# Contrast adjustment on one core: 6 MB tiles of 48 KB rows in place of 4 MB tiles of 32 KB rows, with the clip moved to VectorE

## The chip, the cores and the metric

The kernel runs on one core of a Trainium2 chip. A core has TensorE (matrix products), VectorE, ScalarE and GpSimd (elementwise work and reductions), SyncE (here only an issuer of transfers), and 16 DMA engines that move data between HBM, the chip's memory, and SBUF, the core's own memory of 128 partitions. The metric is the device time of one execution in microseconds, as a median over runs. Lower is better.

## The reference

The input is 48 images (16 batches of 3 channels) of 512 x 512 float32 values. Each image is stretched around its own mean and clipped:

```python
def reference(x, factor):                       # factor = 1.5
    mean = np.mean(x, axis=(2, 3), keepdims=True)
    return np.clip(mean + factor * (x - mean), 0, 1).astype(np.float32)
```

So each output value is clip(factor * x + bias, 0, 1) with bias = (1 - factor) * mean, one bias per image. An image's bias needs the whole image first. Input and output are 50.33 MB each.

## The kernel before

The input is taken as one long row of numbers and cut into 12 tiles of 4 MB. A tile has 128 partitions with 8192 contiguous values each (ROW, 32 KB), so one image covers 32 partitions and a tile holds four whole images. A ring of six such tiles (BUFS) lies in SBUF; tile t lives in buffer t % 6, is changed in place, and is stored from there.

For each tile, `compute(t)` does the following. VectorE sums the first 4352 columns of every partition (L78), while ScalarE sums the other 3840 with an activation that has an accumulator and writes its copy to a scratch tile, junk (L82). TensorE multiplies both sums with a block matrix, blockw, that adds up the 32 partitions of each image and scales by (1 - factor) / pixels (L86, L87); every partition of an image gets its image's bias in PSUM. VectorE copies it to SBUF (L89). Then, in two chunks of 5120 and 3072 columns, ScalarE does relu(factor * x + bias), and VectorE takes the minimum with 1 (L93, L94). Tile 0 has three chunks, and its first 2048 columns are stored on their own.

Loads are issued by SyncE's queue (SP), stores by ScalarE's queue, in the order of the program. SP first issues the loads of the first six tiles: tile 0 in two pieces (1 MB and 3 MB), tile 1, then tiles 2 and 3 together, and 4 and 5 together. From then on it issues load t + 6 behind `compute(t)`; that load waits until store t, which empties its buffer, is complete. ScalarE's store waits for VectorE's last minimum of the tile, and behind it in ScalarE's order are the sums of the next tile. Nothing is ordered by a scheduler: the schedule is manual.

Of the kernel before, what the change touches and what calls it, by code (L numbers as in the profile page):

```python
# [1 line left out]

# [4 lines left out]


P = 128  # L10
ROW = 8192
BUFS = 6
CHUNKS = (5120, 3072)
SHORT = 2048
FIRST = (SHORT, 3072, 3072)
SUM = 4352


@with_exitstack
def kernel(  # L20
    ctx: ExitStack,
    tc: tile.TileContext,
    x: bass.AP,
    factor: float,
    out: bass.AP,
):


    nc = tc.nc
    f32 = mybir.dt.float32  # L30
    Alu = mybir.AluOpType
    Act = mybir.ActivationFunctionType

    B, C, H, W = x.shape
    n_img, n_pix = B * C, H * W
    ppi = n_pix // ROW
    per_tile = P // ppi
    n_tiles = n_img // per_tile
    assert ppi * ROW == n_pix and per_tile * n_tiles == n_img

    factor = float(factor)
    wconst = (1.0 - factor) / float(n_pix)

    x_f = x.rearrange("b c h w -> (b c h w)")
    out_f = out.rearrange("b c h w -> (b c h w)")

    def dram(ap, t, c0=0, c1=ROW):
        return bass.AP(tensor=ap.tensor, offset=t * P * ROW + c0, ap=[[ROW, P], [1, c1 - c0]])

    consts = ctx.enter_context(tc.tile_pool(name="consts", bufs=1))  # L50
    xpool = ctx.enter_context(tc.tile_pool(name="xpool", bufs=1))
    jpool = ctx.enter_context(tc.tile_pool(name="jpool", bufs=1))
    rpool = ctx.enter_context(tc.tile_pool(name="rpool", bufs=2))
    bpool = ctx.enter_context(tc.tile_pool(name="bpool", bufs=2))
    psum = ctx.enter_context(tc.tile_pool(name="psum", bufs=2, space=bass.MemoryType.PSUM))

    blockw = consts.tile([P, P], f32, name="blockw")
    nc.gpsimd.memset(blockw, 0.0)  # L58
    for a in range(0, P, ppi):
        nc.gpsimd.memset(blockw[a : a + ppi, a : a + ppi], wconst)  # L60


    ring = xpool.tile([P, BUFS, ROW], f32, name="ring")

    def load(t, c0=0, c1=ROW, n=1):

        b = t % BUFS
        src = bass.AP(
            tensor=x_f.tensor,
            offset=t * P * ROW + c0,  # L70
            ap=[[ROW, P], [P * ROW, n], [1, c1 - c0]],
        )
        nc.sync.dma_start(out=ring[:, b : b + n, c0:c1], in_=src)  # L73

    def compute(t):
        xt = ring[:, t % BUFS, :]
        sums = rpool.tile([P, 2], f32, name="sums")
        nc.vector.tensor_reduce(  # L78
            out=sums[:, 0:1], in_=xt[:, 0:SUM], axis=mybir.AxisListType.X, op=Alu.add
        )  # L80
        junk = jpool.tile([P, ROW - SUM], f32, name="junk")
        nc.scalar.activation(  # L82
            out=junk, in_=xt[:, SUM:ROW], func=Act.Copy, accum_out=sums[:, 1:2]
        )
        pbias = psum.tile([P, 1], f32, name="pbias")
        nc.tensor.matmul(pbias, blockw, sums[:, 1:2], start=True, stop=False)  # L86
        nc.tensor.matmul(pbias, blockw, sums[:, 0:1], start=False, stop=True)  # L87
        bias = bpool.tile([P, 1], f32, name="bias")
        nc.vector.tensor_copy(out=bias, in_=pbias)  # L89
        c = 0  # L90
        for n in FIRST if t == 0 else CHUNKS:
            part = xt[:, c : c + n]
            nc.scalar.activation(out=part, in_=part, func=Act.Relu, bias=bias, scale=factor)  # L93
            nc.vector.tensor_scalar(out=part, in0=part, scalar1=1.0, scalar2=None, op0=Alu.min)  # L94
            if t == 0 and c == FIRST[0]:
                store(t, 0, c)
            c += n
        store(t, FIRST[0] if t == 0 else 0, ROW)

    def store(t, c0, c1):  # L100
        nc.scalar.dma_start(out=dram(out_f, t, c0, c1), in_=ring[:, t % BUFS, c0:c1])

    with tc.manual_schedule():
        load(0, c1=SHORT)
        load(0, c0=SHORT)
        load(1)
        load(2, n=2)
        load(4, n=2)
        for t in range(n_tiles):
            compute(t)  # L110
            if t + BUFS < n_tiles:
                load(t + BUFS)


# [1 line left out]
_INS = ['x', 'factor']  # L116
_OUTS = [((16, 3, 512, 512), 'float32')]

_NUMBERS = {'factor': 1.5}


# [26 lines left out]
```

## Time and profile before

| what | value |
|---|---|
| median of 7 runs | 239.43 us (239.22 to 239.69) |
| profiled execution, its own time | 239.6 us |
| span in the profile | 237.7 us |
| busy in the span: ScalarE / VectorE / TensorE / GpSimd | 131.1 / 111.9 / 14.0 / 0.9 us |
| moved by DMA | 50.33 MB read, 50.33 MB written, 423 GB/s over the span |
| load queue (q1) / store queue (q10), share of the 16 DMA engines | 49.6% / 49.1% |
| first compute / last store issued | 12.86 us / 217.66 us |

The span is the part of the execution that the profile covers; the rest of the time lies around it. A row of the profile's groups reads: line, engine, operation, output <- input with shapes, count, then the busy time in us and the mean of one in ns, then the idle time of that engine just before, with what ended it. The slices cut the span in 40 equal parts, about 5.9 us each, and a digit is the busy share in tenths. A landing is the time from the issue of a transfer to its completion.

### The profile page before, as it was taken

The page shows a single profiled execution, that of the slowest core. Times are in us where ns is not written, and L with a number is a line of the kernel's source. Part 1 is how long each engine was busy: PE and PEld are TensorE (multiplying, and loading weights), DVE is VectorE, ACT ScalarE, POOL GpSimd, SP SyncE. Part 2 cuts the span into 40 slices and gives each one's busy share as a digit, 9 for nine tenths or more (in the row PEclk, how much of TensorE's full clock was granted, in tenths as well). Part 3 has the DMA queues.
Part 4 walks back from the last instruction along what each step waited for, and adds up shares of the span by engine and source line. Part 5 has one row for each costly group of instructions (what it writes and reads, how often), then busy time and mean ns, then how long its engine had stood idle before and what let it go on. Part 6 is the DMA issues. An engine that isn't in the chain of part 4 may idle for free.

```text
span 237.7 us, 307 instructions
## 1 busy us (share of the span) xinstructions
PE 14.0 (6%) x48; PEld 12.0 (5%) x48; DVE 111.9 (47%) x49; ACT 131.1 (55%) x50; POOL 0.9 (0%) x9
## 2 busy tenths in 40 slices
PE   0010010001010001010010100100100100100000
PEld 0010010001010001010010100100100100100000
DVE  0073846162864343782928739273462643716000
ACT  2058678056679046769676796753671690593000
POOL 1000000000000000000000000000000000000000
DMA  7999999999999999999999999999999999999996
GB/s 288 418 441 441 418 441 354 459 433 442 436 441 436 425 408 425 436 441 441 441 436 441 436 436 430 408 420 441 436 436 441 441 436 436 441 425 413 419 441 265
DMA packets 3713, 100.67 MB, mean 423 GB/s; under 512 B 384, under 2 KB 384, under 8 KB 384
## 3 DMA queue, kind: packets, MB, share of 16 engines
q1 hardware_dynamic: 1840, 50.33, 49.6%
q10 hardware_dynamic: 1872, 50.33, 49.1%
q14 instruction: 1, 0.01, 0.0%
HBM read 50.33 MB, written 50.33 MB: 423 GB/s over the span
## 4 chain that ended last, share of the span: by engine, by line
DMA 57%; DVE 19%; ACT 10%; another core or an unknown queue 3%; issue 1%; PE 1%; SPq 1%; ACTq 0%
DMA ring<-in_x_dram 40%; DMA out_dram<-ring 17%; ACT ring L93 10%; DVE ring L94 9%; DVE sums L78 9%; PE pbias L87 1%; SPq L73 1%; DVE bias L89 0%; ACTq L93 0%
## 5 line engine op out<-in xcount | busy, mean ns | idle before, releaser
L93 ACT ACTIVATE ring<-ring,bias 128x3072 f32<-128x3072 f32 (+2 forms) x25 | 87.9, 3564 | 22.1 <-DVE bias L89 13.2
L94 DVE TENSOR_SCALAR ring<-ring 128x3072 f32<-128x3072 f32 (+2 forms) x25 | 54.3, 2209 | 56.1 <-ACT ring L93 56.1
L78 DVE TENSOR_REDUCE sums<-ring 128x1 f32<-128x4352 f32 x12 | 56.2, 4683 | 41.5 <-DMA ring<-in_x_dram 41.5
L82 ACT ACTIVATE junk<-ring 128x3840 f32<-128x3840 f32 x12 | 40.8, 3402 | 61.9 <-DMA ring<-in_x_dram 48.6
L86 PE MATMUL pbias<-sums,blockw 128*128 128x1 f32 x24 | 7.0, 361 | 190.3 <-ACT junk L82 190.3
L86 PEld LDWEIGHTS pbias<-sums,blockw 128*128 128x128 f32 x24 | 6.0, 311 | 191.2 <-ACT junk L82 174.7
L87 PE MATMUL pbias<-sums,blockw 128*128 128x1 f32 x24 | 7.0, 362 | 3.9 <-DVE sums L78 3.4
L87 PEld LDWEIGHTS pbias<-sums,blockw 128*128 128x128 f32 x24 | 6.0, 310 | 5.0 <-DVE sums L78 5.0
L89 DVE COPY bias<-pbias 128x1 f32<-128x1 f32 x12 | 1.9, 158 | 8.1 <-PE pbias L87 8.1
L82 ACT ACTIVATION_READ_ACCUMULATOR junk<-ring 128x1 f32 x12 | 2.2, 186 | 0.0
L82 ACT ACT_TABLE_LOAD x1 | 1.3, 1283 | 0.7 <-PEq L129 0.7
L60 POOL MEMSET blockw<- 32x32 f32 x4 | 0.5, 117 | 0.2
L58 POOL MEMSET blockw<- 128x128 f32 x1 | 0.2, 204 | 0.3 <-POOLq L129 0.3
L129 POOL MEMSET const-bfloat16-1.0<- 128x1 bf16 x1 | 0.1, 111 | 0.0
L129 POOL MEMSET const-uint8-127<- 128x1 uint8 x1 | 0.1, 111 | 0.0
L129 POOL MEMSET const-float32-1.0<- 128x1 f32 x1 | 0.1, 108 | 0.0
L129 POOL MEMSET const-float32-0.0<- 128x1 f32 x1 | 0.1, 103 | 0.2 <-issue 0.2
## 6 DMA issues: line engine op xcount, KB each, us to landing
out_dram<-ring ACTq DMA_DIRECT2D x11, 4096.0 KB, 37.9
ring<-in_x_dram SPq DMA_DIRECT2D x7, 4096.0 KB, 46.9
ring<-in_x_dram SPq DMA_DIRECT2D x2, 8192.0 KB, 65.7
ring<-in_x_dram SPq DMA_DIRECT2D x1, 3072.0 KB, 11.7
out_dram<-ring ACTq DMA_DIRECT2D x1, 3072.0 KB, 29.8
ring<-in_x_dram SPq DMA_DIRECT2D x1, 1024.0 KB, 4.8
out_dram<-ring ACTq DMA_DIRECT2D x1, 1024.0 KB, 18.8
```

The lines of the kernel that those rows point to most:

```text
L58: nc.gpsimd.memset(blockw, 0.0)
L60: nc.gpsimd.memset(blockw[a : a + ppi, a : a + ppi], wconst)
L73: nc.sync.dma_start(out=ring[:, b : b + n, c0:c1], in_=src)
L78: nc.vector.tensor_reduce(out=sums[:, 0:1], in_=xt[:, 0:SUM], axis=mybir.AxisListType.X, op=Alu.add)
L82: nc.scalar.activation(out=junk, in_=xt[:, SUM:ROW], func=Act.Copy, accum_out=sums[:, 1:2])
L86: nc.tensor.matmul(pbias, blockw, sums[:, 1:2], start=True, stop=False)
L87: nc.tensor.matmul(pbias, blockw, sums[:, 0:1], start=False, stop=True)
L89: nc.vector.tensor_copy(out=bias, in_=pbias)
L93: nc.scalar.activation(out=part, in_=part, func=Act.Relu, bias=bias, scale=factor)
L94: nc.vector.tensor_scalar(out=part, in0=part, scalar1=1.0, scalar2=None, op0=Alu.min)
L129: nc = _bacc.Bacc("TRN2", target_bir_lowering=False, num_devices=1)
```

## The change

The tiles become larger and fewer: 8 tiles of 6 MB, with 12288 contiguous values (48 KB) per partition and four buffers in place of six; the SBUF taken by the ring is the same. A tile now holds six images, and an image covers 21 1/3 partitions: a row consists of three parts of 4096 columns, and the border between two images can lie between two parts of one partition. So the sums are made by part: VectorE reduces columns 0 to 6143 in three sums of 2048, and ScalarE sums 2048 and 4096 columns, in place, without the scratch tile.

The bias becomes a vector of three numbers per partition, one for each part. GpSimd spreads a partition's five sums over three classes with a mask (cls), one matmul with a new blockw adds them over the partitions, and VectorE picks each part's class out of PSUM (a multiplication with the mask pick and a small reduction). GpSimd builds the masks and blockw at the start, out of memsets and affine selects.

ScalarE then does factor * x + bias for the last two parts (4096 columns each; only the last part in the first and the last tile), VectorE for the others, and VectorE clips the whole row of 12288 columns with one instruction, max with 0 and min with 1. In tile 0 the first 2048 columns are clipped and stored on their own, the other 10240 after that.

SP issues tile 0 in one load of 6 MB, then tile 1, then tiles 2 and 3 together; load t + 4 follows `compute(t)` and waits for store t.

```diff
-ROW = 8192
-BUFS = 6
-CHUNKS = (5120, 3072)
-SHORT = 2048
-FIRST = (SHORT, 3072, 3072)
-SUM = 4352
+PART = 4096
+ROW = 3 * PART
+HALF = PART // 2
+BUFS = 4
+FIRST = (HALF, ROW - HALF)
+HEAD = (ROW,)
+IMGS = 6
+CLS = 3
+NSUM = 5
...
-    nc.gpsimd.memset(blockw, 0.0)
-    for a in range(0, P, ppi):
-        nc.gpsimd.memset(blockw[a : a + ppi, a : a + ppi], wconst)
+    pool.memset(blockw, wconst)
...
+        pool.affine_select(
+            out=cols, in_=cols, pattern=[[-3 * period, P // period], [0, p1 - p0]],
+            compare_op=Alu.is_ge, fill=0.0, base=2 - units * first, channel_multiplier=3,
+        )
...
     def compute(t):
         xt = ring[:, t % BUFS, :]
-        sums = rpool.tile([P, 2], f32, name="sums")
+        own = sums[:, t, :]
         nc.vector.tensor_reduce(
-            out=sums[:, 0:1], in_=xt[:, 0:SUM], axis=mybir.AxisListType.X, op=Alu.add
-        )
-        junk = jpool.tile([P, ROW - SUM], f32, name="junk")
-        nc.scalar.activation(
-            out=junk, in_=xt[:, SUM:ROW], func=Act.Copy, accum_out=sums[:, 1:2]
-        )
-        pbias = psum.tile([P, 1], f32, name="pbias")
-        nc.tensor.matmul(pbias, blockw, sums[:, 1:2], start=True, stop=False)
-        nc.tensor.matmul(pbias, blockw, sums[:, 0:1], start=False, stop=True)
-        bias = bpool.tile([P, 1], f32, name="bias")
-        nc.vector.tensor_copy(out=bias, in_=pbias)
+            out=own[:, 0:3], in_=xt[:, 0 : 3 * HALF].rearrange("p (m c) -> p m c", m=3), axis=X,
+            op=Alu.add,
+        )
+        for m, a, b in (3, 3 * HALF, 4 * HALF), (4, 2 * PART, ROW):
+            part = xt[:, a:b]
+            nc.scalar.activation(out=part, in_=part, func=Act.Copy, accum_out=own[:, m : m + 1])
+        pool.tensor_tensor(
+            out=spread[:, t, :].rearrange("p (r m) -> p r m", r=CLS),
+            in0=own[:, None, :].to_broadcast([P, CLS, NSUM]),
+            in1=cls,
+            op=Alu.mult,
+        )
+        nc.tensor.matmul(totals[:, t, :], blockw, spread[:, t, :], start=True, stop=True)
+        nc.vector.tensor_tensor(
+            out=picked[:, t],
+            in0=totals[:, t, :][:, None, :].to_broadcast([P, 3, CLS * NSUM]),
+            in1=pick.rearrange("p k r m -> p k (r m)"),
+            op=Alu.mult,
+        )
+        nc.vector.tensor_reduce(out=bias[:, t, :], in_=picked[:, t], axis=X, op=Alu.add)
+
+
+        kd = 1 if 0 < t < n_tiles - 1 else 2
+        for k in range(kd, 3):
+            third = xt[:, k * PART : (k + 1) * PART]
+            nc.scalar.activation(
+                out=third, in_=third, func=Act.Identity, scale=factor, bias=bias[:, t, k : k + 1]
+            )
         c = 0
-        for n in FIRST if t == 0 else CHUNKS:
-            part = xt[:, c : c + n]
-            nc.scalar.activation(out=part, in_=part, func=Act.Relu, bias=bias, scale=factor)
-            nc.vector.tensor_scalar(out=part, in0=part, scalar1=1.0, scalar2=None, op0=Alu.min)
-            if t == 0 and c == FIRST[0]:
-                store(t, 0, c)
+        for n in FIRST if t == 0 else [ROW]:
+            end = c + n
+            for k in range(kd):
+                a, b = max(c, k * PART), min(end, (k + 1) * PART)
+                if a < b:
+                    part = xt[:, a:b]
+                    nc.vector.tensor_scalar(
+                        out=part, in0=part, scalar1=factor, scalar2=bias[:, t, k : k + 1],
+                        op0=Alu.mult, op1=Alu.add,
+                    )
+            part = xt[:, c:end]
+            nc.vector.tensor_scalar(
+                out=part, in0=part, scalar1=0.0, scalar2=1.0, op0=Alu.max, op1=Alu.min
+            )
+            store(t, c, end)
+            c = end
...
     with tc.manual_schedule():
-        load(0, c1=SHORT)
-        load(0, c0=SHORT)
+        c = 0
+        for n in HEAD:
+            load(0, c, c + n)
+            c += n
         load(1)
         load(2, n=2)
-        load(4, n=2)
```

## The prediction

> **What bounds the kernel now.** I read the slices of the span first, then the DMA queues, then the chain, then the groups of instructions.
>
> ```profile
> DVE  0073846162864343782928739273462643716000
> ACT  2058678056679046769676796753671690593000
> ...
> DMA  7999999999999999999999999999999999999996
> GB/s 288 418 441 441 418 441 354 459 433 442 436 441 436 425 408 425 436 441 441 441 436 441 436 436 430 408 420 441 436 436 441 441 436 436 441 425 413 419 441 265
> ```
>
> The engines have holes everywhere; the DMA row has none between its first and its last slice, at 408 to 459 GB/s almost throughout. Only the ends are cut: 288 and 265.
>
> ```profile
> q1 hardware_dynamic: 1840, 50.33, 49.6%
> q10 hardware_dynamic: 1872, 50.33, 49.1%
> ```
>
> q1 is the loads (SP), q10 the stores (ScalarE). Together they keep the 16 DMA engines busy for 98.7% of 237.7 us, 234.6 us. So the time is: 2.1 us until the first load moves (the chain of waits shows DMA from 2.11), the packets, and the completion at the end. No engine's work is in that sum as long as one of the two queues always has something to do.
>
> ```profile
> 208.53 4.57 ACT ring L93
> 213.10 0.02 issue
> 213.13 4.51 DVE ring L94 x2
> ```
>
> This is the end of the chain of waits. The last store is issued at 217.66 (timeline), and the previous two stores (issued at 178.92 and 198.26) are then still moving, so even the last tile's compute is covered. The chain names engines because it follows one tile; it does not mean that they set the end.
>
> **What the skill says.** (1) The Trainium skill, "DMA: Bandwidth & Descriptors", section "Queues, rings and completion order": each DMA engine takes turns between the queues that have work, a packet at a time. The trace agrees: the short store of tile 0 (8 KB rows beside 32 KB rows of loads) takes 18.8 us to land for 1 MB. (2) Same page, "Why a DMA increments its semaphore by 16 and not by 1": a descriptor moves one contiguous run, and only a row over 64 KiB has to be cut. Here q1 has 1840 packets: 13 tile-sized sets of 128 rows, plus 11 loads times 16 completions (1664 + 176). So one row is one packet at 32 KB; 48 KB is not shown. (3) "VectorE: DVE Perf Modes", "The perf-mode tier table": fp32 tensor_scalar runs at twice the rate of tensor_reduce. The rows below agree (0.52 and 1.08 ns per column). (4) "GPSIMD Engine Reference", 2.1 "Instruction dispatch": the first call to a freshly loaded GpSimd kernel costs about 6 us; no run so far shows it.
>
> **The rows for the costs.**
>
> ```profile
> L78 DVE TENSOR_REDUCE sums<-ring 128x1 f32<-128x4352 f32 x12 | 56.2, 4683 | 41.5 <-DMA ring<-in_x_dram 41.5
> L93 ACT ACTIVATE ring<-ring,bias 128x5120 f32<-128x5120 f32 x11 | 50.2, 4561 | 19.9 <-DVE bias L89 11.0 <-issue 8.9
> L82 ACT ACTIVATE junk<-ring 128x3840 f32<-128x3840 f32 x12 | 40.8, 3402 | 61.9 <-DMA ring<-in_x_dram 48.6 <-DVE ring L94 13.3
> L93 ACT ACTIVATE ring<-ring,bias 128x3072 f32<-128x3072 f32 x13 | 36.8, 2840 | 0.0
> L94 DVE TENSOR_SCALAR ring<-ring 128x5120 f32<-128x5120 f32 x11 | 31.1, 2827 | 51.5 <-ACT ring L93 51.5
> L94 DVE TENSOR_SCALAR ring<-ring 128x3072 f32<-128x3072 f32 x13 | 22.9, 1761 | 2.5 <-ACT ring L93 2.5
> ```
>
> **The change, DMA side (on the path).** The bytes stay. The rows become 48 KB, so there are fewer packets. The trace's own packet records give 309 ns for 8 KB, 912 ns for 24 KB and 1213 ns for 32 KB: 0.0368 ns per byte and about 8 ns per packet. That gives 1816 ns for 48 KB and 1514 ns for 40 KB. Each DMA engine carries 8 rows of every tile. Before: per queue 11 x 8 x 1213 + 8 x (309 + 912) = 116.5 us, both 233.0. After: loads 64 x 1.816 = 116.2; stores 56 x 1.816 + 8 x (0.309 + 1.514) = 116.3; both 232.5. Completion packets fall from 24 to 16 per DMA engine, at 9 ns: 0.07. Sum: -0.6 us. Bounds: -1.1 us (the short-row start of the first load also cost something: its 1 MB lands at 4.8 us where 1.2 + 8 x 0.309 = 3.7) and +0.5 us (rows cut in two, below). The start (SP issues at 0.74) and what follows the last packet stay.
>
> **The change, compute side (covered, if the queues never run dry).** A tile is now 6 MB and goes through, in order: reduce of 6144 columns, 4683 x 6144/4352 = 6.6 us (ScalarE's sums of 2048 + 4096 columns take about 1.9 + 3.6 + 2 x 0.19 = 5.9 beside it); then GpSimd spread, matmul, two small VectorE operations. Before, reduce to first activation was 0.92 us (54.58 to 55.50); one more VectorE operation at 0.16 plus hops and a GpSimd operation that no row shows (0.1 as a memset, to 2 us; I take 0.4) make 1.6. Then two activations of 4096 columns, 7.3 (as 5120 + 3072 columns now, 7.31), beside a 4096-column tensor_scalar at 162 + 0.5205 x 4096 = 2.3; then the clip of 12288 columns, 162 + 0.5205 x 12288 = 6.56. Sum 22.0 us a tile; in the last, with VectorE doing two thirds, 6.6 + 1.6 + 4.6 + 6.6 = 19.3. Both operations of a tensor_scalar, max and min, or a bias from SBUF, are not in the trace; I take the single operation's rate, and twice the time as the other end.
>
> Schedule, with 14.5 us for a tile alone on DMA and 29.1 when the queues alternate. Load 0 lands at 17.5, load 1 at 32. Tile 0 issues its stores at 28.2 (17.5 + 6.6 + 1.6 + 2 x 1.23) and 37.2, tile 1 at 59.2. Loads 2 and 3 are one DMA that lands at about 74, with store 0 in between; load 4 is issued when store 0 is done at 76, and by then store 1 has been queued for 17 us. Tiles 2 to 5 leave at 96, 118, 140, 162, each before the store ahead of it is through (98, 131, 160, 189). Load 7 is issued at 160 when store 3 is done, and lands at 194; tile 6 left at 187. Tile 7 issues its store at 194 + 19.3 = 213, moving by 214.5, while store 6 occupies the queue until 220.5. So nothing runs dry, and the narrowest place is this tail: 6 us of slack. The chain could be some 2.5 to 3 us longer in every tile (9 us of waiting for tile 7, plus 6 of tail, over six tiles), or 6 us in the last, before the time feels it.
>
> GpSimd's setup grows from 5 memsets to some 20 operations, needed at 24 us by the first spread. Load queue and store 1 cover about 10 us of delay there; uncovered, each further us is one. SP's waits are for stores as before; behind a waiting load stand only later loads. ScalarE's store waits for the clip; behind it are the next tile's sums, which could not gain more than their 5.9 us beside a 6.6 us reduce. The removed junk tile, second matmul and PSUM copy were covered and give nothing.
>
> **Rivals.** *A, DMA-bound as now, 0.68:* span 237.1, profiled time 239.0 where 239.6 was, median 239.43 - 0.6 = 238.8, own range 238.3 to 239.3. *B, 48 KB rows go as two packets, 0.07:* 264 data packets per DMA engine instead of 208 at 8 ns, +0.5 us: 239.9. For it, nothing shows 48 KB; against it, the 32 KB rows are whole. *C, the tail runs dry, 0.14:* the chain from landing to store is longer than I sum (GpSimd's spread at 3 us or more, setup late), and past the slack each us is one in the last tile and several when in all: 239.6 to 245. Larger tiles speak for it: in the kernel before, the last tile needs 14.7 us from landing to store, now 19.3. *D, the two-operation tensor_scalar loses its double rate, 0.05:* the clip takes 13 us, a tile 28.4; tile 7 starts at 74 + 5 x 28.4 = 216, stores at 242, and ends 18 us later: 260, slower; it decides from a clip of some 9.5 us on. *E, more than the packets is saved at the start, 0.06:* 237.8 to 238.3.
>
> **How the numbers follow.** A measurement of this kernel can tell about 0.2%, 0.48 us, from no change, and A's gain is close to that: of A's 0.68 I give 0.45 faster, 0.21 same, 0.02 slower. B is 0.03 same, 0.04 slower; C 0.01 and 0.13; D all slower, E all faster. Sum: faster 0.51, same 0.25, slower 0.24. The range 238.1 to 240.6 holds A, B, a third of C and some of E, near 0.8.
>
> **What would show it.** Right: a DMA row without holes, q1 and q10 with 64 x 16 + 112 and 72 x 16 + 144 packets (a few hundred more if B), clip near 6.6 us and GpSimd's spread under 1 us, last load landing near 194, last store issued near 213 and store 6 still moving. Wrong: a slice below 9 in the DMA row near 60 to 80 or 210 to 225, a clip of 13 us, or tile 0 waiting for GpSimd.

## The result, and the profile after

The changed kernel takes 241.19 us at the median (240.11 to 245.18, 12 runs), the kernel before 239.36 us beside it (239.09 to 239.79, 30 runs). The ratio is 1.0074, with a 95% interval of 1.0062 to 1.0086: slower, by 1.8 us, where 0.6 us faster was forecast. The profiled execution took 240.86 us, and its span is 239.0 us, where 237.1 was forecast. The time of the changed kernel also varies more from execution to execution than that of the kernel before. A ratio leaves out executions more than 1.5% above the fastest of their kernel and lies close to the ratio of the means of the others, so long executions weigh more in it than in the medians.

First the slices and the queues of the changed kernel's page:

```profile
DVE  0009899819000963984698199637781908894000
ACT  2009505690000956179346908660758008510000
...
DMA  7999999998999999999999999999999999999993
GB/s 272 477 420 411 444 432 392 446 405 381 474 417 426 461 436 411 428 477 411 403 477 428 403 444 461 411 403 494 420 395 461 444 413 428 469 420 395 477 436 148
...
q1 hardware_dynamic: 1136, 50.33, 49.5%
q10 hardware_dynamic: 1296, 50.33, 48.7%
```

The packets are exactly those forecast: 1136 loads (64 x 16 and 112 completions) and 1296 stores (72 x 16 and 144), so a row of 48 KB is one packet. The DMA row has almost no hole between its ends; its one 8 is in the stretch in which tile 0's stores run. But the busy time is 98.2% of 239.0, 234.7 us, where it had been 234.6 us. The saving of 0.6 us is not there, and the last slice has fallen from 265 to 148 GB/s: something ends raggedly.

Next the groups of instructions, and four rows of the timeline, in order of time (start, duration, engine, line, operation, and in brackets what the engine waited for):

```profile
L129 DVE TENSOR_REDUCE sums<-ring 128x3 f32<-128x6144 f32 x8 | 52.4, 6549 | 46.7 <-DMA ring<-in_x_dram 46.7
L170 DVE TENSOR_SCALAR ring<-ring 128x12288 f32<-128x12288 f32 (+2 forms) x9 | 52.6, 5849 | 30.5 <-ACT ring L155 30.3
L136 POOL TENSOR_TENSOR spread<-sums,cls 128x15 f32<-128x15 f32 x8 | 1.7, 213 | 199.5 <-DVE sums L129 199.5
```

```profile
18.48 6.55 DVE L129 TENSOR_REDUCE sums<-ring 128x3 f32<-128x6144 f32 x1 [18.48 <-DMA ring<-in_x_dram]
...
198.29 6.55 DVE L129 TENSOR_REDUCE sums<-ring 128x3 f32<-128x6144 f32 x1 [7.39 <-DMA ring<-in_x_dram]
...
211.10 6.56 DVE L170 TENSOR_SCALAR ring<-ring 128x12288 f32<-128x12288 f32 x1
217.69 0.34 ACTq L124 DMA_DIRECT2D out_dram<-ring  x1
```

The engines do what was forecast: 6.55 us for the reduce, 6.56 for the clip of 12288 columns (two operations at the full double rate), 0.21 for GpSimd's spread, and 217.69 - 198.29 = 19.4 us from the last landing to the last store, forecast 19.3. What is late are the landings. Tile 0 lands at 18.5 and not at 17.5, tile 7 at 198.3 and not at 194.

The trace's packet records say more. Each of the 16 DMA engines writes a completion when its share of a transfer is done. A transfer has landed when the last engine has. Here are the first and the last completion of tile 0's landing, the first, the mean and the last completion of the last store, and the mean busy time of an engine, all worked out from the packet records in us from the start of the span (compute sees a landing some 0.3 us after the last completion, 18.48 for tile 0):

```
                          tile 0 landed       last store complete            busy, mean
kernel before             12.05 to 12.46      235.55 / 235.84 / 236.59       234.66
changed kernel            16.83 to 18.18      235.65 / 236.15 / 237.82       234.55
```

Before, the engines stand 0.40 us apart when tile 0 is in; now 1.35 us. At the end the last engine is 0.75 us behind the mean before, and 1.66 us now; in the sorted completions it stands alone, 1.0 us after the last but one. The span's 1.2 us (239.0 - 237.7) is 0.3 us of later mean and 0.9 us of the last engine. The records also show the first packets of 48 KB at 2.1 to 3.3 us where the later ones take 1.815, and load packets up to 0.7 us too long while tile 0's stores run, from 33 to 55 us.

### The profile page after: what moved, and what is told of

Read it like the earlier page. It is cut to its first block, busy times and chain, and to the rows that moved or that the text cites. A ratio compares the mean times of both kernels' runs of the same rounds, so it can differ in the third digit from the quotient of the medians.

```text
span 239.0 us, 247 instructions
## 1 busy us (share of the span) xinstructions
PE 4.9 (2%) x16; PEld 4.0 (2%) x16; DVE 131.4 (55%) x44; ACT 97.4 (41%) x47; POOL 5.0 (2%) x30
## 3 DMA queue, kind: packets, MB, share of 16 engines
q1 hardware_dynamic: 1136, 50.33, 49.5%
q10 hardware_dynamic: 1296, 50.33, 48.7%
## 4 chain that ended last, share of the span: by engine, by line
DMA 39%; DVE 32%; ACT 8%; another core or an unknown queue 7%; issue 2%; PE 1%; POOL 0%; POOLq 0%; ACTq 0%; DVEq 0%; SPq 0%
DMA ring<-in_x_dram 22%; DMA out_dram<-ring 17%; DVE ring L170 14%; DVE sums L129 14%; ACT ring L155 8%; DVE ring L165 4%; PE totals L142 1%; DVE picked L143 0%; DVE bias L149 0%; POOL spread L136 0%; POOLq L217 0%; POOLq L136 0%; ACTq L155 0%; DVEq L170 0%
## 5 line engine op out<-in xcount | busy, mean ns | idle before, releaser
L135 ACT ACTIVATE ring<-ring 128x2048 f32<-128x2048 f32 (+1 forms) x16 | 44.1, 2755 | 93.7 <-DMA ring<-in_x_dram 64.4
L129 DVE TENSOR_REDUCE sums<-ring 128x3 f32<-128x6144 f32 x8 | 52.4, 6549 | 46.7 <-DMA ring<-in_x_dram 46.7
L170 DVE TENSOR_SCALAR ring<-ring 128x12288 f32<-128x12288 f32 (+2 forms) x9 | 52.6, 5849 | 30.5 <-ACT ring L155 30.3
L155 ACT ACTIVATE ring<-ring,bias 128x4096 f32<-128x4096 f32 x14 | 51.3, 3702 | 18.3 <-DVE bias L149 18.3
L165 DVE TENSOR_SCALAR ring<-ring,bias 128x4096 f32<-128x4096 f32 (+1 forms) x11 | 23.6, 2158 | 0.3
L142 PE MATMUL totals<-spread,blockw 128*128 128x15 f32 x16 | 4.9, 383 | 201.0 <-POOL spread L136 201.0
L142 PEld LDWEIGHTS totals<-spread,blockw 128*128 128x128 f32 x16 | 4.0, 311 | 201.8 <-POOL spread L136 201.8
L136 POOL TENSOR_TENSOR spread<-sums,cls 128x15 f32<-128x15 f32 x8 | 1.7, 213 | 199.5 <-DVE sums L129 199.5
L135 ACT ACTIVATION_READ_ACCUMULATOR ring<-ring 128x1 f32 x16 | 3.0, 187 | 0.0
L101 POOL TENSOR_SCALAR_AFFINE_SELECT blockw<-blockw 128x42 f32<-128x42 f32 (+2 forms) x5 | 0.9, 219 | 0.0
L97 POOL TENSOR_SCALAR_AFFINE_SELECT blockw<-blockw 128x42 f32<-128x42 f32 (+2 forms) x5 | 0.9, 218 | 0.0
```

What stands on the lines that cost most here:

```text
L97: pool.affine_select(out=cols, in_=cols, pattern=[[-3 * period, P // period], [0, p1 - p0]], compare_op=Alu.is_ge, fill=0.0, base=2 - unit ...
L101: pool.affine_select(out=cols, in_=cols, pattern=[[3 * period, P // period], [0, p1 - p0]], compare_op=Alu.is_gt, fill=0.0, base=units * ( ...
L129: nc.vector.tensor_reduce(out=own[:, 0:3], in_=xt[:, 0 : 3 * HALF].rearrange("p (m c) -> p m c", m=3), axis=X, op=Alu.add,)
L135: nc.scalar.activation(out=part, in_=part, func=Act.Copy, accum_out=own[:, m : m + 1])
L136: pool.tensor_tensor(out=spread[:, t, :].rearrange("p (r m) -> p r m", r=CLS), in0=own[:, None, :].to_broadcast([P, CLS, NSUM]), in1=cls, ...
L142: nc.tensor.matmul(totals[:, t, :], blockw, spread[:, t, :], start=True, stop=True)
```

## The experiments

All compare with the kernel before on the same chip, which stood at 239.3 to 239.4 us each time. "Long executions" are those over 240.8 us; the kernel before had none.

**Four theories.** One run repeats the changed kernel, and three each change one of its constants or one line.

```diff
 # e1_head_split
-HEAD = (ROW,)
+HEAD = (HALF, ROW - HALF)
 # e1_store0_whole
-FIRST = (HALF, ROW - HALF)
+FIRST = (ROW,)
 # e1_last_split
+LAST = (PART, ROW - PART)
...
-        for n in FIRST if t == 0 else [ROW]:
+        for n in FIRST if t == 0 else LAST if t == n_tiles - 1 else [ROW]:
```

> The changed kernel itself, for comparison on one chip. All theories: about 241.2 us. Four theories for the 1.8 us that it lost are named for this and the next three runs. S (start): the first load as one piece of 48 KB rows makes its first packets uneven between the DMA engines (1.8 to 3.3 us where 1.8 is normal); one engine stays late, since each carries a fixed share. M (mix): the short store of tile 0 (8 KB rows) makes the load packets beside it longer, 0.9 us on the mean in the profile after. T (tail): the last store is issued at 217.7 where the store queue empties from 221.5 on; in slower executions it runs dry. P (packets): 48 KB packets as such. T expects this kernel's runs to spread over 1 us or more, and the longest to have the last store after the queue has emptied.

241.12 us (240.08 to 242.06, 6 runs), ratio 1.0075 (1.0053 to 1.0096): the loss is there again, four of six long, and in its profile tile 0's landing is spread over 1.36 us.

> The first load in two pieces, 2048 and 10240 columns, as the kernel before has it in kind. S: the landing of tile 0 spreads by 0.4 us over the engines and not 1.35, and the time falls by 0.5 to 1.0 us to about 240.4. M, T and P: within 0.3 us of 241.2.

239.77 us (239.15 to 244.25, 22 runs), ratio 1.0040 (1.0019 to 1.0060). One transfer of 1 MB ahead takes back 1.35 of the 1.83 us by the medians, about half by the ratios, and the landing of tile 0 is spread over 0.47 us. This is S, at least for a part of the loss. But 8 of the 22 executions are long, and the profiled one is among them (241.73 us).

> Tile 0 is clipped and stored whole, no store with 8 KB rows. M: load packets between 33 and 60 us go back to 1815 ns, the time falls by 0.5 to 1.0 us to about 240.4. S, T and P: within 0.3 us of 241.2.

248.23 us (247.32 to 249.00, 5 runs), ratio 1.0369 (1.0348 to 1.0389). M had the place right and the sign wrong: without the short store it is 7.1 us worse than the changed kernel, not 0.8 better. The load packets are not mended, they are worse. About 1 us of this is a tail that runs dry: the last store is issued at 225.46 and moves at 226.32, when the first engine has been through with the store ahead since 224.51.

> The last tile is clipped and stored in two pieces, 4096 and 8192 columns, so that its first store is issued some 6 us earlier. T: the time falls to about 240.3 and the runs spread less. S, M and P: within 0.3 us of 241.2, since in the profile the queue had not run dry.

240.53 us (240.12 to 242.94, 7 runs), ratio 1.0064 (1.0037 to 1.0090). The interval overlaps that of the changed kernel, so T is not decided here. The slack in the changed kernel is thinner than forecast, though: its last store is issued at 217.69, could move 0.9 us later (225.46 to 226.32 in e1_store0_whole), and the first DMA engine is through with store 6 at 221.15. That is 2.6 us and not 6.

**The start and the long executions.** The same kernel again, with the tail split too, with half rows, and the same question put to the kernel before.

```diff
 # e2_head_last: e1_head_split and e1_last_split together
 # e2_half_rows: on top of e1_head_split, in load() and likewise in store()
-        nc.sync.dma_start(out=ring[:, b : b + n, c0:c1], in_=dram(x_f, t, c0, c1, n))
+        mid = (c0 + c1) // 2
+        cuts = ((c0, mid), (mid, c1)) if c1 - c0 > HALF else ((c0, c1),)
+        for a, e in cuts:
+            nc.sync.dma_start(out=ring[:, b : b + n, a:e], in_=dram(x_f, t, a, e, n))
 # e2_before_whole_head: the kernel before
-        load(0, c1=SHORT)
-        load(0, c0=SHORT)
+        load(0)
```

> The first load in two pieces once more, for a profile of one of the shorter executions and for comparison on one chip. S: most executions at about 239.4 us, as the kernel before, with the end of the last store spread by 0.5 us over the engines; the rest, near 241.7, have one DMA engine that falls back by 1 to 3 us in the middle, through single load packets that take 0.3 to 1.3 us longer (seen in the first profile of this kernel at 148 to 171 us). If S is only part of it, the shorter executions stay above 239.7.

239.56 us (239.27 to 244.90, 14 runs, 4 of them long), ratio 1.0017 (0.9999 to 1.0035). This time the profile is of one of the shorter executions, 239.62 us with a span of 237.6. A table of windows sets it beside the long one of e1_head_split. After the window and its length come the engines' busy times, the clock, the share of the DMA engines and GB/s; a packet counts in the window in which it starts. First the long execution, then the shorter one:

```profile
235.00:236.00 1.00, 0.00 (x0) 0.00 (x0) 0.00 (x0) 0.00 (x0) 0.00 (x0) 1.00 0.12 49
236.00:237.00 1.00, 0.00 (x0) 0.00 (x0) 0.00 (x0) 0.00 (x0) 0.00 (x0) 1.00 0.11 49
```

```profile
235.00:236.00 1.00, 0.00 (x0) 0.00 (x0) 0.00 (x0) 0.00 (x0) 0.00 (x0) 1.00 0.01 0
236.00:237.00 1.00, 0.00 (x0) 0.00 (x0) 0.00 (x0) 0.00 (x0) 0.00 (x0) 1.00 0.00 0
```

One packet of 1.815 us on one of 16 engines is a share of 0.113. So in the long execution a single engine starts one packet in each of the two windows after the other 15 have started their last; in the shorter one nothing starts any more. The packet records don't name the engine, but those of the long execution hold single load packets, at 148, 152, 161 and 170 us, that take 0.2 to 1.2 us too long, 2.2 us together, and between the landings of tiles 5 and 7 (139 and 199 us) one completion falls back from 0.5 to 2.7 us behind the others. It then stays 2.7 us behind the mean in every transfer to the end: no other engine takes over from a late one. In the shorter execution the last engine ends 0.5 us behind the mean.

> The first load in two pieces and the last tile stored in two. S with T (the tail still runs dry where one engine falls back): the longer executions near 241.7 go, median 239.4. S without T: the longer executions stay in the same share of about one in three, since the engine that falls back ends late whatever is issued, median 239.5 to 239.9.

239.67 us (239.53 to 243.09, 13 runs, 2 long), ratio 1.0027 (1.0003 to 1.0050). No gain over the two-piece load alone, and long executions remain, though 2 of 13 are too few to say whether their share fell. The trace of the long execution above speaks against T as well: its last store is issued at 218.59, and the first engine is through with the store ahead at 221.13, so the queue had not run dry.

> The first load in two pieces, and every other tile moved by two transfers of 24 KB rows in place of one of 48 KB rows (128 packets more for each DMA engine at 8 ns, +1.0 us; the tail's last store is in two as well). P (packets of 48 KB are what slips): no executions near 241.7, all within 0.5 us, near 240.3. Not P: executions with one late engine stay, and the median is above 240.5.

240.03 us (239.93 to 240.12, 8 runs, none long), ratio 1.0027 (1.0017 to 1.0037). The page's queues:

```profile
q1 hardware_dynamic: 2416, 50.33, 49.8%
q10 hardware_dynamic: 2448, 50.33, 49.1%
```

98.9% of its span of 238.2 is 235.6 us, against 98.7% of 237.6, 234.5 us, for 48 KB rows: shorter rows cost 1.1 us of DMA time, as 128 packets at 8 ns and 15 completions more for each engine should. But the mean engine's last completion moves by only 0.7 us (from 235.84 to 236.57), 6 ns a packet: the recorded packet times are a little more than the time that a packet costs. No long execution in 8 looks like P, and e4_half_rows_head1 will take that back.

> The kernel before with tile 0 loaded in one piece of 32 KB rows. S: the landing of tile 0 spreads by about 1 us over the engines and the time rises by 0.3 to 1.0 us to about 239.9. Against S: within 0.2 us of the kernel before.

239.62 us (239.39 to 240.34, 21 runs), ratio 1.0012 (1.0005 to 1.0018). The landing of tile 0 spreads over 0.73 us instead of 0.40, so a start in one piece sets the engines apart in the kernel before as well. But it costs only 0.2 us there, which is the outcome named against S, and in the profile the last engine ends 0.76 us behind the mean, as in the kernel before (0.75): this spread is not carried to the end.

**The first store and the first piece.** Four more pairs of constants, on the changed kernel.

```diff
 # e3_head_whole0, e3_head_f1024 and e3_head_f4096
-HEAD = (ROW,)
+HEAD = (HALF, ROW - HALF)
 # of these, e3_head_whole0
-FIRST = (HALF, ROW - HALF)
+FIRST = (ROW,)
 # e3_head_f1024
-FIRST = (HALF, ROW - HALF)
+FIRST = (HALF // 2, ROW - HALF // 2)
 # e3_head_f4096
-FIRST = (HALF, ROW - HALF)
+FIRST = (PART, ROW - PART)
 # e3_head512, with FIRST as it was
-HEAD = (ROW,)
+HEAD = (HALF // 4, ROW - HALF // 4)
```

> The first load in two pieces, and tile 0 stored whole (no rows of 8 KB in a store), which cost 7 us with the first load in one piece. Late engine (the loss came from engines out of step when the first store begins): below 240, at or under the 239.5 of the two-piece load alone. Store shape (the loss came from 48 KB stores beside the pair of loads): 246 or more again, with load packets near 62 and 107 us that are 0.3 to 2 us too long.

246.15 us (245.29 to 247.25, 4 runs), ratio 1.0290 (1.0259 to 1.0322). The engines were in step (0.53 us at tile 0), and most of the loss is there all the same. So a late engine at the start is not its cause; the change of the first store is. That change is of more than the rows: the first store is also larger, and it is issued at 37.24 us where e2_head_again issues its first at 28.36.

> The first load in two pieces, and a first store of 1024 columns (4 KB rows) in place of 2048. The mean excess of the load packets while the first stores run was 0.95 us at 8 KB. If short rows cause it, it grows and the time rises by some 0.3 us to 239.9; if the beginning of a store beside loads causes it whatever its rows, no change (239.5).

242.20 us (242.08 to 242.28, 4 runs), ratio 1.0122 (1.0107 to 1.0138): 2.6 us more than with 8 KB rows, for 4 KB. The loss has the sign of "short rows cause it" and about nine times the size, so that theory does not explain it. Load packets are too long here not only beside the first stores but again at 84 to 92, 120 and 145 us.

> The first load in two pieces, and a first store of 4096 columns (16 KB rows). If short rows cause the excess of 0.95 us, it halves and the time falls by 0.4 us to 239.1, below the kernel before; if longer store rows are what hurts, as with the whole tile, it rises to 240 or more.

239.13 us (238.80 to 239.80, 12 runs, none long), ratio 0.9996 (0.9987 to 1.0005). The expected direction and size; the kernel before is reached.

> The first load in two pieces of 512 and 11776 columns (2 KB rows first). S: what counts is that the first packets are short; the spread over the engines at the landing of tile 0 is 0.5 us or less and the time is within 0.2 us of the 2048-column piece (239.5). If the first piece has to last until the engines are in step (3 us for 2048 columns, under 1 us here), the spread is that of the one-piece load, near 1.4 us, and the time near 241.

241.11 us (240.00 to 242.95, 8 runs, 4 long), ratio 1.0068 (1.0037 to 1.0099). By its time, a first piece with 2 KB rows is as bad as none. Tile 0's landing is spread over 0.77 us, about half of the one-piece load's, and in the profiled execution (242.48 us), a long one, the last engine ends 3.0 us behind the mean. Short first packets alone are not enough; that the first piece has to last is one reading of it, and the spread does not show it (the 1 MB piece left 0.4 to 0.8 us).

How long the load of tiles 2 and 3 takes to land shows the effect of the first stores, since it is on its way while they run. These are the rows of the DMA issues (last column: us from issue to landing) for a first store of the whole row, of 1024, of 2048 (e2_head_again) and of 4096 columns (e4_head_f4096_b, below):

```profile
ring<-in_x_dram SPq DMA_DIRECT2D x1, 12288.0 KB, 82.0
```

```profile
ring<-in_x_dram SPq DMA_DIRECT2D x1, 12288.0 KB, 76.4
```

```profile
ring<-in_x_dram SPq DMA_DIRECT2D x1, 12288.0 KB, 73.2
```

```profile
ring<-in_x_dram SPq DMA_DIRECT2D x1, 12288.0 KB, 72.0
```

The DMA row of e3_head_whole0 has one 8, ahead of its first store, and otherwise no hole until its last slice, and the mean busy time of a DMA engine is 237.6 us for the same bytes. The packets themselves have become longer: loads at 39 to 44, 64 to 69 and 106 to 111 us take up to 1.7 us more than their 1.815.

**What was left open.** Two constants again, and the half rows without the short first piece.

```diff
 # e4_head_f4096_b: as e3_head_f4096
 # e4_head_f6144
-HEAD = (ROW,)
-FIRST = (HALF, ROW - HALF)
+HEAD = (HALF, ROW - HALF)
+FIRST = (ROW // 2, ROW - ROW // 2)
 # e4_head4096_f4096
-HEAD = (ROW,)
-FIRST = (HALF, ROW - HALF)
+HEAD = (PART, ROW - PART)
+FIRST = (PART, ROW - PART)
 # e4_half_rows_head1: e2_half_rows with HEAD as in the changed kernel, so tile 0 is two transfers of 24 KB rows
-HEAD = (HALF, ROW - HALF)
+HEAD = (ROW,)
```

> The first load in two pieces (2048 and 10240 columns) and the first store of 4096 columns once more, in more rounds: if the packets' gain is real once the start and the first stores are mended, 0.1 to 0.6 us under the kernel before; if the last comparison was chance, within 0.1 us of it.

239.07 us (238.85 to 240.16, 21 runs, none long), ratio 0.9995 (0.9987 to 1.0003). Its page, whose profiled execution took 239.0 us:

```profile
span 237.1 us, 249 instructions
...
DMA  7999999899999999999999999999999999999996
GB/s 287 442 464 398 423 415 489 354 522 362 442 442 398 398 522 406 398 406 522 398 398 481 448 398 398 522 406 398 398 531 398 398 457 473 398 398 506 423 398 265
...
q1 hardware_dynamic: 1280, 50.33, 49.7%
q10 hardware_dynamic: 1296, 50.33, 49.1%
```

The last slice is back at 265. All 16 engines complete the last store within 0.4 us (235.40 to 235.84), and their mean busy time is 234.10 us, 0.56 us under that of the kernel before. The span is 237.1 us, the one that was forecast for the changed kernel, but in part by luck: the mean engine ends 0.3 us earlier than in the kernel before where 0.6 was forecast, and the rest is a last engine only 0.3 us behind the mean where it was 0.75. Over many executions it is 0.2 us under the kernel before, with an interval that takes in 1: not shown to be faster.

> The first load in two pieces, the first store of 6144 columns (24 KB rows), the second of as many. If the trouble grows with the store's rows above 16 KB, 240 to 243; if it comes only with a store of the whole tile, 239.2 as with 4096.

239.03 us (238.74 to 241.10, 20 runs, 2 long), ratio 1.0003 (0.9987 to 1.0019). The trouble does not grow steadily with the first store's rows; 4 KB and the whole row are bad, and 16 and 24 KB good.

> The first load in pieces of 4096 and 8192 columns (16 KB rows first), first store of 4096 columns. If what counts is that the first piece lasts until the engines are in step (over 3 us here, as with 2048 columns), 239.2; if its rows have to be short too, a spread of 0.8 us or more at tile 0's landing, and 239.6 to 240.2.

239.45 us (239.11 to 241.15, 12 runs, 1 long), ratio 1.0017 (1.0000 to 1.0033). The spread at tile 0's landing is 0.82 us, and yet the last engine ends only 0.3 us behind the mean in the profile (239.12 us). A longer first piece is no better than the 1 MB one, and a spread of 0.8 us at tile 0 does not by itself make the end late: with e3_head512 it went with 241.1 us, here with 239.45.

> Every tile by two transfers of 24 KB rows, tile 0 too, so that the first transfer has 24 KB rows (with the short first piece ahead it was 240.03). If the length of the first packets makes the late engine, about half of the one-piece start's loss: 240.3 to 240.7. If packets of 24 KB keep the engines in step by themselves: 240.0. If the missing short piece is all: 241 or more.

241.75 us (240.67 to 242.44, 4 runs, 3 long), ratio 1.0110 (1.0088 to 1.0132). Rows of 24 KB without the short first piece lose as much as rows of 48 KB: tile 0's landing is spread over 1.16 us. So P falls: with 24 KB rows the loss can be there, and 48 KB rows with a short first piece and a first store of 16 KB rows had no long execution in 33.

## Why the prediction was wrong

**Right in kind, too large: the packets.** One packet a row, the counts and 1815 ns for 48 KB came as forecast, and so did 0.6 us less busy time, once the start and the first store were set otherwise (e4_head_f4096_b, 234.10 against 234.66 us). But at the 6 ns a packet that e2_half_rows shows at the engines' ends, 72 packets fewer are worth 0.4 us and not 0.6. Rival B did not happen.

**Right: the compute side.** The durations of the large operations, the 22.0 us a tile (38.10 to 60.14 for tile 1), the clip's double rate (no rival D), and GpSimd's setup, over at 4 us with no operation above 0.27 us. The queues of the changed kernel did not run dry, so C as it was described did not happen; the slack in the tail was 2.6 us and not 6.

**Wrong: "The start (SP issues at 0.74) and what follows the last packet stay."** The sum was made for one DMA engine and taken for all 16, with the start of the kernel before left in. The start was changed: the short first load was gone. I had costed that short start only as a possible saving (the lower bound of -1.1 us). What it cost can be worked out from the packet records: how far, in us, the mean engine is behind one that moves the same bytes without a pause at the usual packet lengths, at 20 us (tile 0 is in), at 80 us (tile 0 is stored) and at 235 us, and how far the last engine ends behind the mean:

```
                       20 us    80 us    235 us    last engine
kernel before          2.44     3.11     2.81      0.75
changed kernel         2.83     3.83     3.76      1.66
e2_head_again          2.48     3.55     3.38      0.50
e4_head_f4096_b        2.54     3.25     3.08      0.29
```

So three terms were missing in the changed kernel: 0.4 us at the start, 0.3 us more beside tile 0's stores, and 0.9 us for the last engine, which the sum did not have at all. With the packets' -0.6, of which 0.2 was not there, that is the +1.2 us of the span. Putting the short load back takes away the first of these terms and, in the shorter executions, the last; by the medians it removed 1.35 us of 1.83 (e1_head_split), by the ratios about half there and three quarters in e2_head_again, since long executions remained. With a first store of 4096 columns besides, these were gone too (none in 33), and the kernel before was reached.

**Missing among the rivals** was any in which the DMA row is full and the end still moves. All of mine made time by a dry queue, by more packets or by a slower engine. What would have raised the question was in the trace before: its last engine already ends 0.75 us behind the mean, its first packets take up to 1.0 us too long, and the 1 MB load takes 4.8 us to land where its packets alone explain 3.7:

```profile
ring<-in_x_dram SPq DMA_DIRECT2D x1, 1024.0 KB, 4.8
```

I read the 1.1 us as a cost of short rows.

**Open.** Why a first transfer of 1 MB in 8 KB rows mends the start, and one of 0.25 MB in 2 KB rows does not, was not found. How lateness at the start becomes lateness at the end was not either: a late engine stays late in one long execution, but in e2_before_whole_head and e4_head4096_f4096 a spread at tile 0 did not reach the end. Five first stores gave 239.0 to 246.2 us with the same load start, but a longer one is also issued later (27.2 us for 1024 columns, 37.2 for the whole row), and rows, size and time of issue were not separated; why the packets around it become longer was not found. A first store of 4096 columns with the load in one piece was not run, so it is not shown that the short first load is still needed beside it. And the single engine that falls back in some executions was seen in the records, but what delays it is not in them.

## What to carry to other kernels

Here the DMA row was full from end to end, and the time was that of the last DMA engine and not of the mean. In such a kernel, look at how far apart the 16 completions of a transfer are, at the start and at the end. A small first load was worth 0.2 us in one kernel and about 1 us in the other, though compute did not need it early; it is worth a try, and so is the first store beside running loads in a few shapes. And when an edit rewrites a start or an end that "stays", cost it as a change of its own.

## What the runs showed that was not expected

- With the same bytes and an almost full DMA row, what tile 0's first store was moved the time over 7 us: 4 KB rows 242.2, 8 KB 239.6, 16 KB 239.1, 24 KB 239.0, the whole 48 KB row 246.2 us. Its size and its time of issue changed with the rows.
- A first load in one piece, of 24 or 48 KB rows, spread the 16 DMA engines by 1.2 to 1.7 us at tile 0's landing; 1 MB in 8 KB rows ahead of it left 0.4 to 0.8 us. In the kernel before the same step was 0.73 against 0.40 us and cost 0.2 us.
- A packet's own time was steady to a few ns through most of the span (309, 611, 912, 1213, 1514, 1815 ns for 8 to 48 KB), but in the changed kernel load packets took up to 3.3 us at the start, and in e1_head_split single ones up to 1.2 us more than usual in the middle.
